# Two 1024 x 1024 projections as streamed seven-product steps, with the weights' sums moved ahead and the residual loaded into the gathering tiles

## The chip, the cores and the metric

The kernel runs on one core of a Trainium2 chip. The metric is the device time of one execution in microseconds; three runs of the kernel before gave 1946.44, 1946.65 and 1947.6 us, a median of 1946.65. Engines: PE is TensorE (PEld its weight loads), DVE is VectorE, ACT is ScalarE, POOL is GpSimd, and SP issues most of the DMAs. All data is float32; the matmuls take operands of the format fp32r.

## The reference

A decoder block: a hybrid mixer (a Mamba-2 branch and a gated linear attention branch, merged by gates), cross-attention to 256 memory tokens, a SwiGLU FFN, with a residual add after each and norms ahead. 1024 tokens, 1024 channels, D_FF 2816. What matters here is the end of the mixer and the beginning of the cross-attention:

```python
merged = sigmoid(g_ssd) * (y_ssd @ w_up_ssd) + sigmoid(g_gla) * (y_gla @ w_up_gla)
h = h + merged @ w_o                               # output projection
n = rmsnorm(h, norm_xattn)
q = (n @ w_xq).reshape(B, S, 4, 256)               # query projection
s = einsum('bshd,bmhd->bhsm', q, k) * 256 ** -0.5  # k, v from the memory, made earlier
o = einsum('bhsm,bmhd->bshd', softmax(s), v).reshape(B, S, 1024) @ w_xo
h = h + o
h = h + (silu(n2 @ w_g) * (n2 @ w_u)) @ w_ffn_out
```

## The kernel before, in words

Activations lie channels x tokens. A float32 product is made from three fp32r matmuls: each operand is split into a high part (`ACT.activation` with Copy) and the rest (a DVE subtraction), and high x high, high x low, low x high are summed in PSUM (`split`).

Large matrix products (input projections, FFN) run in the Strassen-Winograd form: both operands are cut into quarters, seven products B11, B21, T1, B22, T2, T3, T4 of quarters or of sums of quarters give the four quarters of the result. Sums of the down weights `w_ffn_out` are made early by `presum` on POOL: for each of 11 row blocks it loads 1 MB into the one tile `pre`, makes four sums of 128 x 512 and stores each to `down_d`, as steps of a generator that runs beside other stages.

The five projections `w_up_ssd`, `w_up_gla`, `w_o`, `w_xq`, `w_xo` don't use that form. `dense` (called with 0 to 4) walks over 8 blocks of output channels and two halves of the tokens; each of the 16 outputs is one PSUM bank (`acc`) and 8 blocks x 3 matmuls, 384 matmuls of 128x128 by 128x512 in all. Its weights come through `Left`, which loads 1024 x 256 pieces into "aux" slots and splits one block of 128 columns at a time into a ring of two `wd` tiles. Its right operands are eight pairs of high and low tiles (`hl`) that the stage before fills through its `post`:

- `dense(1)` (`w_up_gla`) gates, adds and splits each result into `i_wo` (`post_yg`);
- `dense(2)` (`w_o`) adds the residual, which `quad_of(xT_d)` loads two blocks ahead into tiles `ga`, stores to `h1_d`, scales and splits into `i_xq` (`put_xq`), and squares and adds up for the norm (`s1.take`; POOL or DVE, as `either` chooses by a meter of their queues);
- `dense(3)` (`w_xq`) splits its results into `i_q`. Beside it `s1.close` sums the squares over channels with tiny matmuls, and POOL raises to the power -1/2 (`rstd`), from which the softmax scale `xsc` comes;
- attention goes over 4 heads x 2 token halves (scores, transposes, values) and fills `i_xo`; its keys and values (`kvhl`) are loaded and split by `load_kv`. `dense(4)` (`w_xo`) follows, and then the FFN.

`run(main, (side, rate), ...)` interleaves the program order of a main generator with side generators. The Tile framework then schedules each engine's instructions by priority against its own model of times, with slots allotted as they come free (pools of slots: 14 "op", 4 "aux", 4 "m", each 8 KB a partition); `ahead()` raises the priority. PSUM has four `acc` and four `bank` banks.

## Time and profile before

| | |
|---|---|
| median of three runs | 1946.65 us (1946.44 to 1947.6) |
| profiled execution, first to last instruction | 1949.0 us |
| TensorE busy | 1916.2 us, 98% |
| DVE, ACT, POOL busy | 1298.5, 845.8, 557.8 us |
| granted TensorE clock | 0.998 |
| DMA | 317.98 MB, mean 163 GB/s |
| first matmul of the five projections | 801.9 us |
| attention's first matmul | 1156.5 us |

Durations of matmuls in the profile overlap (they are pipelined, and their ends modelled), so that the time of many matmuls is read from the start of the first to the start of the one after the last. A line of the profile can be a helper's, L73 above all: there the names of the tiles tell operations apart. In an answer by tile, "x40: 1211/1225/2319" are the count and the least, median and greatest duration in ns; in a group, "| 11.9, 1493 |" are busy us and mean ns; in a timeline, the two first numbers are start and duration in us.

### The profile page before, as it was taken

The page shows a single profiled execution, that of the slowest core. Times are in us where ns is not written, and L with a number is a line of the kernel's source. Part 1 is how long each engine was busy: PE and PEld are TensorE (multiplying, and loading weights), DVE is VectorE, ACT ScalarE, POOL GpSimd, SP SyncE. Part 2 cuts the span into 40 slices and gives each one's busy share as a digit, 9 for nine tenths or more (in the row PEclk, how much of TensorE's full clock was granted, in tenths as well). Part 3 has the DMA queues.
Part 4 walks back from the last instruction along what each step waited for, and adds up shares of the span by engine and source line. Part 5 has one row for each costly group of instructions (what it writes and reads, how often), then busy time and mean ns, then how long its engine had stood idle before and what let it go on. Part 6 is the DMA issues. An engine that isn't in the chain of part 4 may idle for free.

```text
span 1949.0 us, 26264 instructions
## 1 busy us (share of the span) xinstructions
PE 1916.2 (98%) x9776; PEld 1615.6 (83%) x9776; DVE 1298.5 (67%) x1873; ACT 845.8 (43%) x1485; POOL 557.8 (29%) x428
## 2 busy tenths in 40 slices
PE   7999999999999999999999999999999999999998
PEld 7998787888878888788887888888888888888888
DVE  7766879877776764655534237677777777766566
ACT  7534564655553444643223235444333333345243
POOL 0012334345543231022433000006445544320002
PEclk9999999999999999999999999999999999999999
DMA  9423383446553653997675201442233224177463
GB/s 341 144 93 101 130 307 107 152 161 186 174 173 123 198 167 124 348 346 270 226 269 164 82 22 44 140 141 82 90 126 110 82 100 144 42 271 239 157 224 126
DMA packets 237875, 317.98 MB, mean 163 GB/s; under 512 B 16538, under 2 KB 156036, under 8 KB 237748
## 3 DMA queue, kind: packets, MB, share of 16 engines
q1 hardware_dynamic: 236020, 310.01, 47.4%
q10 hardware_dynamic: 1728, 6.29, 0.8%
q8 instruction: 77, 1.26, 0.3%
q14 instruction: 50, 0.41, 0.1%
HBM read 215.27 MB, written 100.99 MB: 162 GB/s over the span
## 4 chain that ended last, share of the span: by engine, by line
PE 43%; DMA 3%; POOL 2%; DVE 1%; issue 1%; ACT 1%; POOLq 0%; SPq 0%; DVEq 0%; ACTq 0%
PE acc L51 38%; PE bank L51 4%; DMA pre<-in_w_ffn_out_dram 1%; POOL pre L73 1%; DMA down_d<-pre 1%; PE bank L55 1%; POOL ssum L73 0%; DVE hl L73 0%; POOL sa L73 0%; DMA h_d<-ga 0%; DMA ga<-vm_d 0%; DVE wd L73 0%; ACT wd L227 0%; ACT sq L493 0%; DVE phl L73 0%
## 5 line engine op out<-in xcount | busy, mean ns | idle before, releaser
L51 PE MATMUL acc<-hl,wd 128*128 128x512 f32 x1920 | 440.4, 390 | 3.6 <-DVE wd L73 2.0
L51 PEld LDWEIGHTS acc<-hl,wd 128*128 128x128 f32 x1920 | 359.6, 188 | 80.7 <-DVE wd L73 3.3
L73 DVE TENSOR_TENSOR wlo<-raw,whi 128x512 fp32r<-128x512 f32 x272 | 236.4, 875 | 103.6 <-ACT whi L227 103.5
L227 ACT ACTIVATE whi<-raw 128x512 fp32r<-128x512 f32 x272 | 169.5, 629 | 247.6 <-PE acc L51 201.0
L73 DVE TENSOR_TENSOR o<-acc,o 128x512 f32<-128x512 f32 (+1 forms) x256 | 172.6, 676 | 108.8 <-PE acc L51 95.4
L51 PE MATMUL acc<-fs 128*128 128x512 f32 (+1 forms) x792 | 155.7, 356 | 0.1
L51 PEld LDWEIGHTS acc<-fs 128*128 128x128 f32 x792 | 130.7, 189 | 20.8 <-issue 0.5
L73 DVE TENSOR_TENSOR fs<-fr,fs 128x1024 fp32r<-128x1024 f32 (+1 forms) x84 | 98.9, 1217 | 36.5 <-ACT fs L227 36.4
L227 ACT ACTIVATE fs<-fr 128x1024 fp32r<-128x1024 f32 (+1 forms) x84 | 79.2, 982 | 95.9 <-PE acc L51 31.2
L73 POOL TENSOR_TENSOR raw<-raw,sa 128x512 f32<-128x512 f32 x44 | 57.1, 1297 | 207.8 <-DVE wlo L73 207.8
L73 POOL TENSOR_TENSOR sa<-raw 128x512 f32<-128x512 f32 x43 | 69.6, 1619 | 107.0 <-DMA raw<-in_w_in_dram 78.9
L227 ACT ACTIVATE whi<-sa 128x512 fp32r<-128x512 f32 x96 | 59.6, 626 | 93.7 <-PE acc L51 92.3
L73 DVE TENSOR_TENSOR wlo<-sa,whi 128x512 fp32r<-128x512 f32 x96 | 80.9, 843 | 13.7 <-ACT whi L227 12.7
L73 DVE TENSOR_TENSOR wd<-raw,wd 128x1024 fp32r<-128x1024 f32 x40 | 52.8, 1323 | 47.6 <-ACT wd L227 47.2
L73 POOL TENSOR_TENSOR rstd<-rstd,mhalf 128x4 f32<-128x4 f32 (+1 forms) x7 | 8.7, 1246 | 257.0 <-DVE rstd L73 257.0
L227 ACT ACTIVATE wd<-raw 128x1024 fp32r<-128x1024 f32 x40 | 42.2, 1057 | 90.4 <-PE acc L51 89.8
L51 PE MATMUL acc<-T4h,whi 128*128 128x512 f32 x192 | 76.3, 397 | 2.4 <-DVE o L73 2.4
L51 PE MATMUL acc<-B22h,wlo 128*128 128x512 f32 x192 | 75.7, 394 | 1.5 <-DVE wlo L73 1.5
L51 PE MATMUL acc<-T1h,whi 128*128 128x512 f32 x192 | 76.3, 397 | 0.0
L51 PE MATMUL acc<-T2h,whi 128*128 128x512 f32 x192 | 75.9, 395 | 0.0
L51 PE MATMUL acc<-T3h,whi 128*128 128x512 f32 x192 | 75.9, 395 | 0.0
L51 PE MATMUL acc<-B22h,whi 128*128 128x512 f32 x192 | 75.7, 394 | 0.0
(399 smaller groups left out, 4698.6 us busy)
## 6 DMA issues: line engine op xcount, KB each, us to landing
raw<-in_w_in_dram SPq DMA_DIRECT2D x26, 1024.0 KB, 5.9
raw<-in_w_ffn_in_dram SPq DMA_DIRECT2D x22, 1024.0 KB, 6.5
act_d<-o SPq DMA_DIRECT2D x77, 256.0 KB, 2.1
fr<-act_d SPq DMA_DIRECT2D x35, 512.0 KB, 7.9
pre<-in_w_ffn_out_dram SPq DMA_DIRECT2D x11, 1024.0 KB, 10.0
fr<-down_d SPq DMA_DIRECT2D x20, 512.0 KB, 3.9
down_d<-pre SPq DMA_DIRECT2D x33, 256.0 KB, 3.1
h_d<-ga SPq DMA_DIRECT2D x32, 256.0 KB, 3.1
```

What stands on the lines that cost most here:

```text
L51: return s.e.matmul(o, x, y, **kw)
L55: return s.e.transpose(o, x, i)
L73: return f(*a, **kw)
L227: ACT.activation(hi, src, AF.Copy)
```

## The change

`w_o` and `w_xq` become instances of a new class `Wide`: seven products in the order B11, T1, B22, T2, B21, T3, T4, each of 512 x 512 x 512 quarters over all channels. A product has two steps of 24 matmuls (4 blocks of output rows x 2 blocks of the sum x 3 terms), four PSUM banks at a time. Four `acc` banks keep a running sum from B11 through T2 and T3 to T4; four `bank` banks hold T1 + B22, and then B21. The quarters of the right operand stay in float32 in four `rq` tiles, are combined in place on DVE (`COMB`) and split step by step together with the streamed weights (`ws`). Weights come as 1 MB quarters, either from the matrix or from sums that `presum` now makes for `w_o` and `w_xq` ahead of the down weights (8 steps more; in program order the last 30 of all its sub-steps now stand beside attention). With `base`, the tile that gathers a quarter (`wk`) is first loaded with the residual, and each evacuation adds to it (`scalar_tensor_tensor` with 0.5). `post_yg` and `put_xq` write float32 quarters and no longer split. `kv_side` loads and splits the first head's keys and values beside the query projection; those of the other heads move from "m" to "op" slots. `w_xo` gets a `Left` of its own, started beside the query projection.

```diff
     down_d = dram("down_d", 4 * D_FF // 2, HALF)
+    wos_d = dram("wos_d", 2 * D, HALF)
+    xqs_d = dram("xqs_d", 2 * D, HALF)
     kT_d = dram("kT_d", D, MEM)
...
     JS = (0, 1)
+    class Wide:
+        SEQ = ("B11", "T1", "B22", "T2", "B21", "T3", "T4")
+        LEFT = {"B11": (0, 0), "B21": (0, 1), "T1": 0, "B22": 3, "T2": 1, "T3": 2, "T4": (1, 1)}
+        COMB = {"T1": ((0, 0), (0, 1), (0, 0)), "T2": ((0, 0), (1, 1), (0, 0)), "T3": ((0, 1), (1, 1), (0, 1)),
+                "T4": ((1, 0), (1, 0), (0, 0))}
+        RIGHT = {"B11": (0, 0), "B22": (1, 1), "B21": (1, 0), "T1": (0, 0), "T2": (0, 0), "T3": (0, 1), "T4": (1, 0)}
+        OUT = {"B11": (0, 0), "T1": (1, 1), "B22": (0, 1), "T2": (0, 1), "B21": (0, 0), "T3": (1, 1), "T4": (1, 0)}
+        def __init__(s, W, sums_d, post, keys, side, base=None, scale=1.0, two=None):
+            s.W, s.sums_d, s.post, s.keys, s.side, s.base, s.scale = W, sums_d, post, keys, side, base, scale
+            s.two = two or (lambda ap: DVE)
+            s.q, s.raw, s.ops, s.keep, s.chain = {}, [], [], {}, None
+        def quad(s, i, j):
+            if (i, j) not in s.q:
+                s.q[i, j] = slot("op", (P, 4, HALF), name="rq")
+            return s.q[i, j]
+        def load(s, n):
+            while len(s.raw) < min(n, 7):
+                src = s.LEFT[s.SEQ[len(s.raw)]]
+                if isinstance(src, tuple):
+                    i, j = src
+                    w = s.W[half(j), half(i)]
+                else:
+                    w = s.sums_d[half(src), :]
+                r = slot(s.keys[len(s.raw)], (P, 4, HALF), name="wr")
+                SP.dma_start(r, w.rearrange("(k p) c -> p k c", p=P))
+                s.raw.append(r)
+        def home(s, i, j):
+            if (i, j) not in s.keep:
+                k = s.keep[i, j] = slot(s.side[len(s.keep)], (P, 4, HALF), name="wk")
+                if s.base is not None:
+                    SP.dma_start(k, s.base[half(i), half(j)].rearrange("(u p) c -> p u c", p=P))
+            return s.keep[i, j]
+        def prep(s, n):
+            while len(s.ops) < min(n, 14):
+                m, kp = divmod(len(s.ops), 2)
+                s.load(m + 1)
+                name, c = s.SEQ[m], slice(2 * kp, 2 * kp + 2)
+                x = [slot("op", (P, 2, 2, HALF), F32R, name="ws") for _ in range(2)]
+                with ahead():
+                    if name in s.COMB:
+                        o, a, b = (s.quad(*ij)[:, c] for ij in s.COMB[name])
+                        sub(s.two(o), o, a, b)
+                    split(s.raw[m][:, c], x[0][:, 0], x[0][:, 1])
+                    split(s.quad(*s.RIGHT[name])[:, c], x[1][:, 0], x[1][:, 1])
+                s.ops.append(x)
+        def evac(s, name, u, p):
+            i, j = s.OUT[name]
+            o = p if name == "T4" and s.base is None else s.home(i, j)[:, u]
+            first = name in ("B11", "T1", "B22")
+            with ahead():
+                if s.base is not None:
+                    DVE.scalar_tensor_tensor(o, p, s.scale, o, ALU.mult, ALU.add)
+                elif first:
+                    ACT.activation(o, p, AF.Copy)
+                elif name != "T4":
+                    add(DVE, o, p, o)
+                if not first:
+                    s.post(i, j, u, o)
+        def steps(s):
+            x = 0
+            for m, name in enumerate(s.SEQ):
+                if name in ("B11", "T1", "B21"):
+                    banks = [(acc if name == "B11" else bank)() for _ in range(4)]
+                    if name == "B11":
+                        s.chain = banks
+                elif name in ("T2", "T3", "T4"):
+                    banks = s.chain
+                fresh = name in ("B11", "T1", "B21")
+                if s.base is not None:
+                    for z in s.SEQ[m:m + 2]:
+                        s.home(*s.OUT[z])
+                for kp in range(2):
+                    s.load(m + 3)
+                    s.prep(x + 3)
+                    w, b = s.ops[x]
+                    for u in range(4):
+                        for k in range(2):
+                            for n, (a, c) in enumerate(((0, 0), (0, 1), (1, 0))):
+                                PE.matmul(banks[u], w[:, a, k, u * P:(u + 1) * P], b[:, c, k],
+                                          start=fresh and kp + k + n == 0, stop=kp + k == 2 and n == 2,
+                                          skip_group_check=True)
+                    x += 1
+                    if kp:
+                        for u in range(4):
+                            s.evac(name, u, banks[u])
+                    yield
     class Left:
...
             return s.w[n]
-    left = Left((t["w_up_ssd"], t["w_up_gla"], t["w_o"], t["w_xq"], t["w_xo"]))
+    left = Left((t["w_up_ssd"], t["w_up_gla"]))
     def paired(keys):
...
         split(src, x[:, 0, half(j)], x[:, 1, half(j)], e)
-    def dense(no, ins, post, pre=lambda o, j: None, js=JS):
+    def dense(no, ins, post, pre=lambda o, j: None, js=JS, left=left):
         todo = [(o, j) for o in range(NB) for j in (js if o + 1 < NB else js[::-1])]
...
     EVEN, ODD = ("op",) * 8, ("op",) * 6 + ("aux",) * 2
-    i_ys, i_yg, i_wo, i_xq, i_q, i_xo = (paired(x) for x in (EVEN, ODD, EVEN, ODD, EVEN, EVEN))
+    i_ys, i_yg, i_q, i_xo = (paired(x) for x in (EVEN, ODD, EVEN, EVEN))
     def fetch(src, dst, gain=None):
...
     s1 = Stats(rp)
+    wides = (("w_o", wos_d), ("w_xq", xqs_d), )
     def presum():
         r = slot("m", (P, 2, D), name="pre")
-        for k in range(KP):
-            SP.dma_start(r, t["w_ffn_out"][256 * k:256 * k + 256, :].rearrange("(j p) c -> p j c", p=P))
+        todo = [(t[w].rearrange("(j k p) c -> k p j c", j=2, p=P)[k], d, 4, k) for w, d in wides for k in range(4)]
+        todo += [(t["w_ffn_out"][256 * k:256 * k + 256, :].rearrange("(j p) c -> p j c", p=P), down_d, KP, k)
+                 for k in range(KP)]
+        for src, dst, kn, k in todo:
+            SP.dma_start(r, src)
             yield
...
             s1_ = sums["m"].tile([P, HALF], F32, name="sa", tag="sa", bufs=2)
-            put = lambda n, ap: SP.dma_start(down_d[(n * KP + k) * P:(n * KP + k + 1) * P, :], ap)
+            put = lambda n, ap: SP.dma_start(dst[(n * kn + k) * P:(n * kn + k + 1) * P, :], ap)
             add(POOL, s1_, a(1, 0), a(1, 1))
...
         gated(g, p)
-        add(either(g), g, g, y)
-        into(i_wo, o, j, g)
+        q = wo.quad(o // 4, j)[:, o % 4]
+        add(either(g), q, g, y)
+    def post_wo(i, j, u, q):
+        o = 4 * i + u
+        SP.dma_start(h1_d[o * P:(o + 1) * P, half(j)], q)
+        put_xq(o, j, q, col("norm_xattn", o))
+        s1.take(j, q)
+    wo = Wide(t["w_o"], wos_d, post_wo, ("aux",) * 7, ("m", "m", "m", "aux"), xT_d, 0.5)
+    def wide_side(x, n):
+        for _ in range(n):
+            yield
+        x.load(2)
+        yield
+        x.prep(1)
+        yield
+        x.prep(2)
+        yield
     def residual(store, stats, gain, put, scale=1.0):
...
         return post
+    xq = Wide(t["w_xq"], xqs_d, lambda i, j, u, p: into(i_q, 4 * i + u, j, p), ("aux", "m", "aux") * 3, ("m", "aux", "aux"))
     def put_xq(o, j, q, g):
-        x = hl(i_xq, o)
-        h, l = x[:, 0, half(j)], x[:, 1, half(j)]
-        ACT.activation(h, q, AF.Copy, scale=g)
-        DVE.scalar_tensor_tensor(l, q, g, h, ALU.mult, ALU.subtract)
+        ACT.activation(xq.quad(o // 4, j)[:, o % 4], q, AF.Copy, scale=g)
     def waiting(g, n):
...
     early = presum()
-    run(dense(0, i_ys, post_ys, lambda o, j: gate(gs_d, o, j)), (fetch_gated(yg_d, sr_d, i_yg), 1.0), (waiting(early, 12), 1.0))
-    run(dense(1, i_yg, post_yg, lambda o, j: (gate(gg_d, o, j), quad(ysg_d, o * P, 0, j))), (early, 1.1))
-    run(dense(2, i_wo, residual(h1_d, s1, "norm_xattn", put_xq, 0.5), quad_of(xT_d)), (early, 1.1))
+    run(dense(0, i_ys, post_ys, lambda o, j: gate(gs_d, o, j)), (fetch_gated(yg_d, sr_d, i_yg), 1.0), (waiting(early, 8), 1.0))
+    run(dense(1, i_yg, post_yg, lambda o, j: (gate(gg_d, o, j), quad(ysg_d, o * P, 0, j))), (early, 1.5),
+        (wide_side(wo, 11), 1.0))
+    run(wo.steps(), (early, 1.3))
     kv = []
-    def load_kv(h):
+    def fetch_kv(h):
         es = [rp.tile([P, 2, 256], F32, name="ga", tag="ga") for _ in range(2)]
-        h_ = slot("m" if h < 3 else "op", (P, 2, 4, 256), F32R, name="kvhl")
         SP.dma_start(es[0], kT_d[h * 256:(h + 1) * 256, :].rearrange("(i p) m -> p i m", p=P))
         SP.dma_start(es[1], vm_d[:, h * 256:(h + 1) * 256].rearrange("(i p) c -> p i c", p=P))
+        return es
+    def split_kv(es, pin=lambda x: x):
+        h_ = slot("op" if kv else "m", (P, 2, 4, 256), F32R, name="kvhl")
         for i in range(2):
-            split(es[i], h_[:, 0, 2 * i:2 * i + 2], h_[:, 1, 2 * i:2 * i + 2])
+            pin(ACT.activation(h_[:, 0, 2 * i:2 * i + 2], es[i], AF.Copy))
+            pin(sub(DVE, h_[:, 1, 2 * i:2 * i + 2], es[i], h_[:, 0, 2 * i:2 * i + 2]))
         kv.append(h_)
+    def load_kv(h):
+        split_kv(fetch_kv(h))
     xsc = cp.tile([P, NCH], F32, name="xsc")
...
         yield
-    run(dense(3, i_xq, lambda o, j, p, g: into(i_q, o, j, p)), (xq_side(), 1.0), (early, 1.0))
-    drain(early)
-    load_kv(0)
+    def kv_side():
+        for _ in range(2):
+            yield
+        es = fetch_kv(0)
+        for _ in range(9):
+            yield
+        split_kv(es, pinned)
+        yield
+    left_xo = Left((t["w_xo"],))
+    def next_left():
+        left_xo.upto(2)
+        yield
+    run(xq.steps(), (xq_side(), 1.0), (early, 1.0), (kv_side(), 1.0), (waiting(next_left(), 12), 1.0))
     u_xo_stats = Stats(rp)
...
             a.score(1)
+        for _ in range(3):
+            next(early, None)
+    drain(early)
     rbc2 = u_xo_stats.sum
...
     B = Operands(b_xo, 4, order=("B11", "T1", "B21", "B22", "T2", "T3", "T4"))
-    for n, _ in enumerate(dense(4, i_xo, residual(h2_d, u_xo_stats, "norm_ffn", put_xo), quad_of(h1_d), js=(1, 0))):
+    for n, _ in enumerate(dense(0, i_xo, residual(h2_d, u_xo_stats, "norm_ffn", put_xo), quad_of(h1_d), js=(1, 0), left=left_xo)):
         if n >= 8:
...
         if n == 12:
```

## The prediction

> **What bounds the kernel now.** I read the page's busy shares first, then the 40 slices, then the chain, then the stages by windows.
>
> ```profile
> span 1949.0 us, 26264 instructions
> PE 1916.2 (98%) x9776; PEld 1615.6 (83%) x9776; DVE 1298.5 (67%) x1873; ACT 845.8 (43%) x1485; POOL 557.8 (29%) x428
> PE   7999999999999999999999999999999999999998
> ...
> 1320.48 459.26 PE acc L51 x2026
> ```
>
> TensorE is full in all but the first and last slice, and the chain that ended last runs on it: 2026 matmuls of 512 columns in 459.26 us, 226.7 ns each. That, and not the 390 ns that the groups print (pipelined, ends modelled), is the price of one matmul. The profiled execution (1949.0 us) stands 2.35 us above the median of 1946.65.
>
> The two stages that change are the third and fourth of the five dense projections. Their place on TensorE, by the timeline and the windows (busy us of PE, PEld, DVE, ACT, POOL; then clock, DMA share, GB/s):
>
> ```profile
> 869.68 161.78 PE L51 MATMUL acc<-hl,wd 128*128 128x512 f32 x713
> 1031.84 0.73 PE L51 MATMUL acc<-hl,wd 128*128 128x512 f32 x2 [0.38 <-ACT wd L227]
> 1033.34 21.60 PE L51 MATMUL acc<-hl,wd 128*128 128x512 f32 x94 [0.76 <-DVE wd L73]
> 1055.09 0.73 PE L51 MATMUL acc<-hl,wd 128*128 128x512 f32 x2
> 1056.60 17.97 PE L51 MATMUL acc<-hl,wd 128*128 128x512 f32 x78 [0.78 <-DVE wd L73]
> 1074.73 9.36 PE L51 MATMUL acc<-hl,wd 128*128 128x512 f32 x40 [0.15 <-DVE hl L73]
> ...
> 1087.23 69.42 PE L51 MATMUL acc<-hl,wd 128*128 128x512 f32 x305
> 1156.50 7.96 PE L51 MATMUL acc<-kvhl,hl 128*128 128x256 f32 x65
> L51 PE MATMUL bank<-ones,ssum x16: 164/208/251, 1083.9 to 1087.1; 128*128 128x1 f32 x16
> ```
> ```profile
> 200.00:450.00 250.00, 246.08 (x1206) 201.17 (x1206) 207.06 (x244) 136.91 (x221) 103.78 (x78) 1.00 0.52 176
> 889.00:976.00 87.00, 87.00 (x386) 72.04 (x385) 48.51 (x54) 23.31 (x33) 34.81 (x24) 1.00 0.73 252
> 976.00:1063.00 87.00, 84.93 (x371) 69.09 (x370) 34.67 (x38) 24.58 (x36) 31.27 (x23) 1.00 0.66 220
> 1087.00:1156.00 69.00, 69.00 (x306) 57.14 (x306) 15.43 (x20) 13.05 (x19) 1.01 (x1) 1.00 0.14 46
> 1156.00:1221.00 65.00, 64.61 (x404) 57.16 (x404) 46.03 (x117) 38.81 (x102) 0.00 (x0) 1.00 0.10 33
> 1700.00:1880.00 180.00, 180.00 (x804) 149.01 (x803) 117.13 (x126) 78.85 (x91) 18.56 (x10) 1.00 0.64 221
> ```
>
> Counting back from 1156.5 us, where attention begins, 768 matmuls (two projections of 384) reach to about 977.1 us. The two stages take 179.3 us; 768 x 0.2267 = 174.1 us of it is matmul. Of the other 5.2 us, 1.5 us go to the sixteen tiny matmuls of the statistics (1083.9 to 1087.2 us), and 3.7 us are waits, mostly for a split weight (wd). The granted clock is 1.00. DVE and ACT have much room here before the change: 34.67 and 24.58 us of 87, then 15.43 and 13.05 of 69.
>
> **The change, part by part.**
>
> *Matmuls.* A projection was 8 x 2 outputs x 8 blocks x 3 terms = 384 matmuls. It becomes 7 products x 4 rows x 4 blocks x 3 = 336 of the same form (128x128 stationary, 128x512 moving). Two projections lose 96: 96 x 0.2267 = 21.8 us, all on the path. The old 3.7 us of waits go with the old streaming. Ceiling of the gain: 25.5 us (179.3 - 672 x 0.2267 - 1.5). What takes their place is the question.
>
> [...]
>
> *Operands of the steps.* Each projection has 14 half-products, and each splits 1024 elements a partition of weights and as many of activations: 28 splits. Each T product also combines two quarters first, 2 x 4 = 8 subtractions of the same width, all on DVE.
>
> ```profile
> L227 ACT ACTIVATE wd<-raw x40: 1039/1061/1065, 800.8 to 1275.2; 128x1024 fp32r<-128x1024 f32 x40
> L73 DVE TENSOR_TENSOR wd<-raw,wd x40: 1211/1225/2319, 803.2 to 1276.3; 128x1024 fp32r<-128x1024 f32 x40
> L73 DVE SCALAR_TENSOR_TENSOR ga<-acc,ga 128x512 f32<-128x512 f32 x13 | 8.9, 683 | 12.2 <-PE acc L51 12.2
> L493 ACT ACTIVATE sq<-ga 128x512 f32<-128x512 f32 x10 | 6.2, 622 | 25.2 <-POOL ssum L73 25.2
> L227 ACT ACTIVATE hl<-acc x16: 576/590/602, 1075.5 to 1157.4; 128x512 fp32r<-128x512 f32 x16
> L73 DVE TENSOR_TENSOR hl<-acc,hl x16: 679/686/692, 1076.1 to 1159.3; 128x512 fp32r<-128x512 f32 x16
> L1368 ACT ACTIVATE hl<-ga,cols x16: 707/723/727, 986.0 to 1071.4; 128x512 fp32r<-128x512 f32 x16
> L73 POOL TENSOR_TENSOR ssum<-ssum,sq x14: 1282/1344/1590, 1010.9 to 1072.7; 128x512 f32<-128x512 f32 x14
> ```
>
> Output projection, 76.2 us of matmul (336 x 0.2267). DVE: 28 splits + 8 combinations at 1.225 = 44.1, 28 evacuations at 0.683 = 19.1, together 63.2 us undisturbed. ACT: 28 x 1.06 = 29.7, plus 16 scalings at 0.723 and 16 squares at 0.62, 51 us: no bound. Query projection: DVE 44.1 + 12 additions from PSUM (8.2) + 16 splits of the result at 0.686 (11.0) + the first keys' two (1.4) = 64.7 us; ACT 28 x 1.06 + 12 copies and 16 splits at about 0.59 = 46 us. So DVE rises from about 40% to about 84% of these stages before any disturbance. The gated projection before them loses its 16 splits of i_wo (11 us of DVE) and gets the first two half-products' operands (5 us).
>
> *The sums' POOL work.* Sums of w_o and w_xq add 8 steps of four POOL additions to the 11 of the down weights; every step also issues 1 load and 4 stores on SP, 40 issues more in all at 0.32 to 0.43 us spread over 300 us, and 16 MB of traffic.
>
> ```profile
> 833.98 1.28 POOL L73 TENSOR_TENSOR sa<-pre 128x512 f32<-128x512 f32 x1 [47.69 <-DMA pre<-in_w_ffn_out_dram]
> L73 POOL TENSOR_TENSOR pre<-pre x22: 1272/1733/2359, 836.6 to 1025.6; 128x512 f32<-128x512 f32 x22
> 956.87 2.16 POOL L73 TENSOR_TENSOR sa<-pre 128x512 f32<-128x512 f32 x1 [8.56 <-issue]
> ...
> 1005.81 1.28 POOL L73 TENSOR_TENSOR sa<-pre 128x512 f32<-128x512 f32 x1 [14.29 <-DMA h_d<-ga]
> ```
>
> The first step's sums start at 834 us. Four steps start from 956.87 to 1005.81, three periods of 16 us; a single buffer makes load, sums and stores take turns. The first steps are slower (834, 865, 893 us), and 16 more periods from 893 reach about 1155: beside attention, where POOL is idle (0.00 of 65 us). The sums of w_o are done by about 915 us, 60 us before use; those of w_xq by about 980, 80 us before use. Cost on the path: 0, with that cover. Takes and the small power on POOL queue behind a step's 5.2 us; the softmax scale waits for them and has some 40 us to spare (under PSUM below).
>
> What POOL does to DVE is not free:
>
> ```profile
> 944.85 3.46 POOL L73 TENSOR_TENSOR pre<-pre 128x512 f32<-128x512 f32 x2
> 947.07 2.32 DVE L73 TENSOR_TENSOR wd<-raw,wd 128x1024 fp32r<-128x1024 f32 x1
> L73 DVE TENSOR_TENSOR wd<-raw,wd 128x1024 fp32r<-128x1024 f32 x8 | 11.9, 1493 | 0.2 <-ACT wd L227 0.2
> ```
>
> A split of 1.225 us took 2.32 beside POOL, and the mean in the gated stage (889 to 976, POOL busy 40%) was 1.493. The new stages put 36 such subtractions in 76 us beside about 30 us of sums and, in the first, 14 takes (19 us). At +0.27 us each DVE would need 73 us in the first and 74 in the second, at 1.5 times that disturbance 78 and 77. Against 76.2 that is just full; two half-products are prepared before the first stage starts.
>
> Stall from this, bounded: below 0 us (1700:1880, streamed operands of the same build, no loss at 65% DVE); above 12 us (rival 1). Between: 200:450, where DVE is 83% busy, lost 3.9 of 250 us, 1.6%, or 2.4 us on 152. I take twice that, 5 us, since DVE comes out fuller here than there.
>
> *PSUM.* Four banks hold the running sum from B11 to T4, four serve T1/B22 and B21. B22 writes T1's banks and T4 writes T3's, so each waits for an evacuation; between a bank's last matmul and its next lie 18 matmuls, 4.1 us, against 0.68 us of evacuation and at most one or two operations ahead of it. Taken as 0; it costs if DVE runs late, which the 5 us hold. The statistics' matmuls now find no free bank until B22 ends, 33 us into the query stage: what waits for them is the scale, needed 43 us on.
>
> *Residual in the gathering tiles.* 16 quarter-block loads become 4 loads of 1 MB, at least 7 us ahead of need; a buffer for the first comes free 11 us before the gated stage ends. 0.
>
> *Traffic.* Output stage: weights and sums 7, residual 4, h1 4, sums' steps about 9 MB, 24 MB in 76 us, 315 GB/s, against 220 now.
>
> ```profile
> GB/s 396 402 405 380 397 385 396 404 407 310 218 242 186 332 290 253 246 238 367 119 236 223 314 218 158 231 319 210 188 323 377 215 229 344 309 115 142 159 54 187
> pre<-in_w_ffn_out_dram SPq DMA_DIRECT2D x11, 1024.0 KB, 10.0
> ```
>
> This row (800 to 1063) shows about 400 GB/s sustained at its start, so 315 fits, and a 1 MB operand that lands in 10 us is asked for three products (33 us) ahead. Bounds 0 and 2 us (the first stage starts its sums earlier in the full part); I take 0.
>
> *Boundaries.* B11 and T1 need only the upper channels, finished half a stage earlier; each later quarter is ready two products before use. Attention's first head needs the quarters of T2 and B21. Gain or loss 0, to 5 us of loss (rival 2). Beside attention POOL now runs: DVE's 46 us of 65 mostly read PSUM; 0 to 2 us, taken 0.
>
> Sum: -21.8 - 3.7 + 5 = -20.5 us: 1949.0 becomes 1928.5, and the median 1926.2.
>
> **The rivals.**
>
> 1. *DVE and POOL take turns and DVE becomes the bound.* If every two-input subtraction and every POOL addition exclude one another, the first stage needs 44.1 + 18 (14 takes at 1.285) + 25.7 (five steps of four) = 87.8 us of turns, 11.6 over; the second 45.5 + 25.7 = 71.2, none over. With the 2.4 us as above the gain is 11.5: 1935.1. For it: the 2.32 us row. Against it: in the gated stage the measured delay was 0.27 us, not a whole POOL operation, and sums can slip, as nobody waits for them. [...]
>
> 2. *Handover to attention.* The scores need acc banks, all held to T4's end, and T4 is evacuated through 4 splits behind T3's 8 DVE operations (8 x 0.686 = 5.5 us). If TensorE waits this out, 1931. Against: those have 10.9 us of T4 itself to drain.
>
> 3. *Slower: SP's queue.* SP issues in order, and a store of a sum waits for POOL; the 14.29 us row shows POOL itself held 14 us by a store. If a product's operand can be issued only once a step (16 us) and a product lasts 10.9, 14 products lose 14 x 5.1 = 71 us: 1926 + 71 - 5 = 1992. It decides from 1.8 us a product (25.5 / 14). Against: the same queue with the same steps cost 3.7 us in the window before, and operands are asked for three products ahead.
>
> 4. *No gain:* the freed TensorE time returns as waits of 20 us or more, 1946.
>
> **How the numbers follow.** Forecast 0.60, rival 1 0.20, rival 2 0.09, rival 3 0.07, rival 4 0.04 (mostly within 0.2%, about what a measurement of this kernel can tell from no change). The likeliest case's own range is 1921 (no stall) to 1931; the range of 8 in 10 reaches from 1920.5 to 1937 to take in rivals 1 and 2. Faster 0.90, same 0.03, slower 0.07.
>
> **What would show it.** 672 matmuls of the new form, 226 to 228 ns apart, in 154 to 162 us between the gated projection and the scores; DVE near 90% there with split means of 1.4 to 1.6 us; TensorE waits on splits or evacuations of 3 to 8 us in total; the sums' last POOL operation between 1120 and 1190 us. It is wrong if TensorE's waits in these stages pass 12 us, if one product waits for its operand's DMA, or if attention takes over 68 us.

## The result, and the profile after

The changed kernel is slower: 1965.59 us (median of four, 1955.8 to 1969.61) against 1947.12 us of the kernel before beside it; ratio 1.0082, 95% interval 1.0055 to 1.0109. The forecast was 1926.2 us. The profiled execution is the fastest of the four, 1955.8 us with a span of 1954.1, so its rows show less than the usual loss; e0 below shows a usual one.

The profile after: totals, and the slices of TensorE, the granted clock and POOL.

```profile
span 1954.1 us, 26262 instructions
PE 1902.8 (97%) x9680; PEld 1599.1 (82%) x9680; DVE 1382.9 (71%) x1927; ACT 881.4 (45%) x1521; POOL 609.0 (31%) x454
PE   7999999999999999999997999999999999999998
POOL 0012333345443221023235540006444444320002
PEclk9999999999999999999999998999999999999999
```

The 96 matmuls are gone (9776 to 9680), and TensorE is no longer full in slice 22 (1026 to 1075 us). By stage, from first matmuls (profiled executions): up to the streamed stages 974.8 us against 977.1 (-2.3); the two streamed stages 184.3 against 179.4 (+4.9); attention and `w_xo` 143.2 against 140.5 (+2.7); the rest 651.8 against 652.0. The matmuls alone would fill 153.8 us of the 184.3 (672 at 0.2267 us, and 1.5 us of statistics). TensorE's timeline there (start, duration, in brackets the idle time ahead and what ended it):

```profile
974.82 8.32 PE L51 MATMUL acc<-ws 128*128 128x512 f32 x36
...
998.23 0.49 PE L51 MATMUL acc<-ws 128*128 128x512 f32 x1 [1.49 <-ACT ws L229]
1000.91 3.03 PE L51 MATMUL acc<-ws 128*128 128x512 f32 x8 [2.19 <-DVE ws L73]
...
1055.57 14.03 PE L51 MATMUL acc<-ws 128*128 128x512 f32 x51 [8.55 <-ACT sq L495]
1071.07 0.50 PE L51 MATMUL acc<-ws 128*128 128x512 f32 x1 [1.47 <-DVE wk L73]
...
1145.32 12.70 PE L51 MATMUL acc<-ws 128*128 128x512 f32 x48 [3.54 <-DVE wk L73]
1159.12 6.12 PE L51 MATMUL acc<-kvhl,hl 128*128 128x256 f32 x49 [1.10 <-DVE hl L73]
```

The largest stop, 8.55 us ahead of the output projection's T4, is put down to ACT's squares. The four engines just before it:

```profile
1047.60 2.28 DVE L73 TENSOR_TENSOR ws<-rq,ws 128x1024 fp32r<-128x1024 f32 x1
1048.76 3.46 POOL L73 TENSOR_TENSOR pre<-pre 128x512 f32<-128x512 f32 x2
...
1052.18 1.26 POOL L73 TENSOR_TENSOR ssum<-ssum,sq 128x512 f32<-128x512 f32 x1
1053.47 0.63 ACT L495 ACTIVATE sq<-wk 128x512 f32<-128x512 f32 x1 [5.89 <-POOL ssum L73]
1054.13 0.69 DVE L73 TENSOR_TENSOR ssum<-ssum,sq 128x512 f32<-128x512 f32 x1 [4.25 <-ACT sq L495]
1054.74 1.28 DVE L73 SCALAR_TENSOR_TENSOR wk<-acc,wk 128x512 f32<-128x512 f32 x2
```

A take is the addition of a square to the norm's sum. Read upward: the evacuation of T3 at 1054.74 stands on DVE behind a take; that take waits for ACT's square, and the square for the only `sq` tile, which a take on POOL still reads; the take on POOL stands behind a step of the sums. TensorE waits for POOL through two engines.

Windows of the same trace (length; busy us of PE, PEld, DVE, ACT, POOL; clock, DMA share, GB/s):

```profile
974.80:1159.10 184.30, 164.05 (x689) 131.74 (x687) 144.06 (x135) 88.64 (x118) 91.77 (x54) 0.94 0.74 265
1159.10:1302.30 143.20, 141.14 (x737) 119.46 (x738) 93.70 (x186) 71.01 (x154) 5.10 (x4) 1.00 0.29 96
1047.00:1056.00 9.00, 0.45 (x2) 0.46 (x2) 4.75 (x5) 2.35 (x4) 6.88 (x5) 0.65 1.02 364
1056.00:1062.00 6.00, 6.00 (x19) 4.71 (x19) 1.92 (x4) 4.00 (x7) 3.13 (x3) 0.68 1.01 352
1062.00:1068.00 6.00, 6.00 (x28) 4.96 (x27) 3.31 (x4) 3.19 (x5) 3.28 (x4) 1.00 0.50 191
```

The fourth row is the tail of the stop: 19 matmuls in 6 us where 26 fit, at a granted clock of 0.68. This stop of 8.6 us costs 1.7 us more by its tail, and in the fifth row the clock is back at 1.00. All waits of TensorE in the two stages add up to 20.3 us. The first row gives the rest of the loss: its matmuls keep TensorE busy for 164.05 us at a clock of 0.94, where 153.8 would do, and these 10.2 us are in the main the tails of all the stops together. Behind the smaller stops the same trace has a clock of 0.95 from 1004 to 1016 us, 0.85 from 1074 to 1084 and 0.78 from 1146 to 1152.

### The profile page after: what moved, and what is told of

Its sections match the earlier page's. It is cut to its first block, busy times and chain, and to the rows that moved or that the text cites. A ratio compares the mean times of both kernels' runs of the same rounds, so it can differ in the third digit from the quotient of the medians.

```text
span 1954.1 us, 26262 instructions
## 1 busy us (share of the span) xinstructions
PE 1902.8 (97%) x9680; PEld 1599.1 (82%) x9680; DVE 1382.9 (71%) x1927; ACT 881.4 (45%) x1521; POOL 609.0 (31%) x454
## 4 chain that ended last, share of the span: by engine, by line
PE 42%; DMA 2%; DVE 2%; POOL 2%; issue 2%; ACT 0%; POOLq 0%; DVEq 0%; SPq 0%; ACTq 0%
PE acc L51 36%; PE bank L51 6%; DMA pre<-in_w_ffn_out_dram 1%; POOL pre L73 1%; DMA down_d<-pre 1%; DVE ws L73 1%; PE bank L55 1%; DVE hl L73 0%; POOL ssum L73 0%; POOL sa L73 0%; DVE wk L73 0%; DVE kvhl L73 0%; DVE wd L73 0%; DVE yt L73 0%; DMA xqs_d<-pre 0%
## 5 line engine op out<-in xcount | busy, mean ns | idle before, releaser
L229 ACT ACTIVATE whi<-raw 128x512 fp32r<-128x512 f32 x272 | 169.5, 629 | 251.0 <-PE acc L51 207.2
L51 PE MATMUL acc<-hl,wd 128*128 128x512 f32 x1152 | 263.8, 390 | 1.9 <-ACT wd L229 1.4
L51 PEld LDWEIGHTS acc<-hl,wd 128*128 128x128 f32 x1152 | 215.5, 188 | 48.4 <-ACT wd L229 2.6
L51 PE MATMUL acc<-ws 128*128 128x512 f32 x384 | 96.4, 410 | 18.4 <-ACT sq L495 8.6
L51 PEld LDWEIGHTS acc<-ws 128*128 128x128 f32 x384 | 75.8, 199 | 37.1 <-ACT sq L495 8.9
L73 POOL TENSOR_TENSOR sa<-pre 128x512 f32<-128x512 f32 x19 | 28.0, 1472 | 231.2 <-DMA pre<-in_w_o_dram 94.3
```

The source lines that it names most:

```text
L51: return s.e.matmul(o, x, y, **kw)
L73: return f(*a, **kw)
L229: ACT.activation(hi, src, AF.Copy)
```

## The experiments

Theories: *coupling* (POOL's sums hold products up, by way of SP's queue and of the square tile), *DVE* (it is simply full), *traffic* (DMA is full). In the expectations, A is the coupling by the square tile and D the one by SP's queue, B is DVE, and C is a late operand at the first stage's start. "Stages" are the two streamed stages, "attention" is attention and `w_xo`; both are us of the one profiled execution, which can stand apart from the median: by 9.8 us below it in after, and by 9.4, 4.8 and 3.8 us above it in e7, e8 and e10.

| kernel | median | ratio to before, 95% | stages | attention |
|---|---|---|---|---|
| before | 1947.12 to 1949.48 beside the others | | 179.4 | 140.5 |
| after | 1965.59 | 1.0055 to 1.0109 | 184.3 | 143.2 |
| after again (e0) | 1966.1, one | | 192.3 | 143.2 |
| e1 takes on DVE | 1965.6 | 1.0072 to 1.0107 | 191.7 | 143.2 |
| e2 no sums | 1939.74 | 0.9938 to 0.9968 | 167.3 | 143.3 |
| e3 sums later | 1948.97 | 0.9990 to 1.0009 | 168.3 | 151.7 |
| e4 = e3 + e1 | 1941.57 | 0.9946 to 0.9976 | 161.1 | 150.5 |
| e5 only `w_o` | 1955.47 | 1.0023 to 1.0050 | 185.6 | 140.0 |
| e6 only `w_xq` | 1954.47 | 1.0012 to 1.0041 | 94.7, query alone | 143.1 |
| e7 = e1 + own queue | 1950.23 | 0.9991 to 1.0024 | 167.7 | 154.3 |
| e8 = after + own queue | 1957.42 | 1.0033 to 1.0067 | 169.5 | 155.8 |
| e9 = e4 + own queue | 1949.16 | 0.9991 to 1.0011 | 154.2 | 159.1 |
| e10 = e4 + stores on own queue | 1948.35 | 0.9986 to 1.0006 | 162.6 | 158.3 |
| e11, few beside attention | 1941.06 | 0.9945 to 0.9969 | 160.4 | 150.9 |
| e12 = e11 + own queue | 1957.28 | 1.0023 to 1.0052 | 154.2 | 160.6 |
| e13 = e4 + softmax scale on ACT | 1937.48 | 0.9918 to 0.9945 | 161.2 | 141.9 |
| e14 = e4, no sums | 1936.52 | 0.9915 to 0.9940 | 164.7 | 143.1 |

**e2, the sums' POOL work taken away.** The kernel leaves out the 44 additions of the down weights: their steps store what they loaded, with the same bytes on the same queue.

```diff
+            if dst is down_d:
+                for n in range(4):
+                    SP.dma_start(dst[...], a(n // 2, n % 2))
+                    yield
+                continue
```

> Leaves out POOL's four sums in each of the 11 steps of the down weights (the pieces are stored as loaded, same bytes, so the FFN's last product is not the reference's); the sums of w_o and w_xq stay. Theory A: POOL's takes no longer stand behind sums, gain 10 to 13 us, about 1953. Theory B: DVE's subtractions fall from up to 2.3 us to 1.22 us, and the query stage's stops (about 6 us) go as well: A and B together about 1945 to 1948. Theory C: 6 us at the start of the first stage stay, since the traffic is the same; without C about 1940.

e2 is 26 us faster than after and 5 us below what A and B together were expected to bring, though DMA moves more per second in the stages (304 GB/s against 265). POOL's 44 additions, which nobody reads for 500 us, decide the sign. One stop of 6.95 us stays, at 1004, for the first stage's third operand.

**e1, the takes on DVE.**

```diff
-                    add(either(q), dst, dst, q)
+                    add(DVE if s.on_dve else either(q), dst, dst, q)
```

> The adds of the squares for the norm in these two stages go to DVE alone (14 adds), POOL keeps only the sums of weights. Theory A (one square tile shared by takes on POOL and on DVE: an evacuation on DVE stands behind an add that waits for ScalarE's square, which waits for POOL's take, which stands behind the sums): the 8.6 us stop ahead of T4 and the slow clock after it go, 10 to 13 us, so about 1953 against the changed kernel's 1965.6. Theory B (DVE is over-full because POOL's sums block its two-input subtractions): DVE gets 5 us more to do, no gain, 1965 or more. Theory C (operands of the first stage land late): the 6 us at the stage's start stay in any case.

The stop ahead of T4 goes, and a longer one appears in the query stage, so that the time stays at 1965.6 us. POOL, DVE, SP, ACT and TensorE in e1's timeline:

```profile
1067.57 17.10 POOL L73 TENSOR_TENSOR sa<-pre 128x512 f32<-128x512 f32 x1 [13.35 <-DMA h_d<-wk]
1084.74 1.30 POOL L73 TENSOR_TENSOR pre<-sa,pre 128x512 f32<-128x512 f32 x1
```
```profile
1082.30 1.22 DVE L73 TENSOR_TENSOR ws<-rq,ws 128x1024 fp32r<-128x1024 f32 x1
```
```profile
1059.86 2.18 SPq L1465 DMA_DIRECT2D h_d<-wk  x4
1084.69 0.32 SPq L1412 DMA_DIRECT2D down_d<-sa  x1
...
1091.88 0.38 SPq L1223 DMA_DIRECT2D wr<-in_w_xq_dram  x1
```
```profile
1099.60 1.06 ACT L229 ACTIVATE ws<-wr 128x1024 fp32r<-128x1024 f32 x1 [18.73 <-DMA wr<-in_w_xq_dram]
```
```profile
1101.19 4.11 PE L51 MATMUL bank<-ws 128*128 128x512 f32 x11 [14.42 <-ACT wk L1255]
```

A POOL addition of 1.3 us lasted 17.10. DVE ran two-SBUF-input operations without a break from 1066 on; the last began at 1082.30 and took 1.22, and POOL ended 1.15 us behind it: one addition. Meanwhile the sum's store stood at the head of SP's queue, SP issued nothing for 22 us, and a product's weights, queued behind that store, were asked for at 1091.88. ACT waited for them until 1099.60; the evacuation `wk` that the last row names stands behind that split on ACT, and TensorE stood still for 14.42 us.

**e0, the changed kernel again**, unedited.

> The changed kernel once more, for a second trace: its profiled execution (1955.8 us) was the fastest of its four times, the others 1964 to 1968. Theory 'queue': the missing 10 us are a stop of 10 to 15 us in the query stage, with a single POOL addition of 10 us or more and a weight operand issued only behind its store, as with the takes on DVE; then this execution, if it is slow, shows such a stop. Theory 'spread': no new stop, but all of the present ones (8.6, 3.5, 2.2 us) a few us longer and a lower clock. A time near 1955 with the known stops tells nothing.

At 1966.1 us it stands with the slower three of the first four, and it shows the long addition without any edit:

```profile
L73 POOL TENSOR_TENSOR sa<-pre x19: 1278/1291/13874, 830.6 to 1169.6; 128x512 f32<-128x512 f32 x19
```

(the first trace's greatest is 2354). SP issued nothing from 1092.8 to 1111.3. The stop itself was shorter than expected, 5.38 and 1.73 us, with a clock of 0.53 from 1138 to 1146 us. The stop ahead of T4 is there too, 7.91 us.

**e5 and e6, one projection alone.** The other one stays in the old form.

```diff
-wides = (("w_o", wos_d), ("w_xq", xqs_d), )
+wides = (("w_o", wos_d), )      # e5;  e6: (("w_xq", xqs_d), )
```

> Only the output projection is streamed; the query projection is as before the change. 48 matmuls fewer (10.9 us) than the kernel before. Theory B (DVE over-full beside POOL's sums) and theory C: the output stage loses what it lost in the changed kernel (about 5 us at its start, 10 us ahead of T4), so 1948 to 1954, no gain over the kernel before. If the two stages only fail together (DVE never gets even), about 1940.

> Only the query projection is streamed; the output projection is as before, where DVE is 40% busy. 48 matmuls fewer, 10.9 us. Theory B: the query stage alone has DVE at about 85% undisturbed beside one sums' step in 15 us, it loses 2 to 6 us: 1941 to 1945. Theory D (a sum's store on SP's queue waits for POOL, POOL is shut out by DVE's row of two-input subtractions, and operands wait behind that store: the 14.4 us stop of the run with the takes on DVE): a stop of this kind can come here too, then 1950 or more.

Each alone is slower than before. e5 has the first mechanism (6.04 us ahead of T4, by way of POOL's take), e6 the second: a POOL addition of 10.10 us in a row of DVE subtractions, the store behind it, and a stop of 15.04 us. Attention stays at 140.0 us in e5 and is 143.1 in e6, as in the changed kernel (143.2), so these 2.7 us come with the streamed query projection.

```profile
1077.39 10.10 POOL L73 TENSOR_TENSOR sa<-pre 128x512 f32<-128x512 f32 x1 [7.49 <-DMA pre<-in_w_ffn_out_dram]
```
```profile
1102.11 4.17 PE L51 MATMUL bank<-ws 128*128 128x512 f32 x11 [15.04 <-ACT wk L1255]
```

**e3 and e4, the same work at another time.** In program order the sums of `w_o` and `w_xq` stand sooner (rate 2.0), no step of the down weights stands beside the streamed stages, and their 55 sub-steps were meant for attention and `w_xo`, with a second load tile. e4 adds e1's edit.

```diff
-    run(wo.steps(), (early, 1.3))
+    run(wo.steps())
-    run(xq.steps(), (xq_side(), 1.0), (early, 1.0), ...
+    run(xq.steps(), (xq_side(), 1.0), ...
```

> No step of the down weights beside the two stages: w_o and w_xq are summed beside the gated projections, the down weights from attention to the next projection, with two load tiles from the third round on. Takes stay where they were. Theories A and B: both causes are gone, about 1945 as for the run without POOL's sums. Theory C: the first stage has 9 MB less traffic and no store ahead of its operands in the queue, so 6 us more, about 1935 to 1940. If attention suffers from POOL, its stretch (143 us from the first score to the FFN in the changed kernel) grows by what is missing.

> The two edits together: sums of the down weights later, and the takes on DVE alone. Theory A: with no sums on POOL the chain through POOL costs at most a take (1.3 us), so within 3 us of the run with the sums later. [...] If it is over 4 us faster, ScalarE's and DVE's waiting for POOL's takes is a cost of its own.

The traces differ from the program order: in both, three steps of the down weights still run in the output projection, where their loads were free to go (POOL is busy for 26.46 us from 976.2 to 1060 us in e4), and none runs beside the query projection. In e4 the stages have only two stops, 1.91 and 2.03 us near their start, and e4 beats both kernels. e3 against e4 isolates the takes (7.2 us of stage time). But attention pays: 150.5 us against 143.

**e7 to e10, the sums' DMAs on POOL's own queue** (e10 the stores alone).

```diff
-            SP.dma_start(r, src)
+            nc.gpsimd.dma_start(r, src)
-            put = lambda n, ap: SP.dma_start(...)
+            put = lambda n, ap: nc.gpsimd.dma_start(...)
```

> Takes on DVE as in the first run, and the loads and stores of the sums are issued from POOL's own queue in place of SP's. Theory D: no operand waits behind a sum's store, so the 14.4 us stop and its slow clock go, and the 4 us at the first stage's start with them: 1965.6 - 20 = about 1943 to 1947. Theory B alone: DVE is as full as before, POOL has more to do, 1965 or more.

> The changed kernel with the sums' DMAs on POOL's own queue, the takes as they were (either engine). Theory D alone: about 1950, since the stop ahead of T4 through the takes (8.6 us) stays and the queue's stops go. Theory A and D both at work: 5 to 12 us slower than the run with both edits. Theory B alone: 1965 or more.

> e4 (sums later, takes on DVE), and the sums' loads and stores issued from POOL's queue, not SP's. Theory 'queue': the two stops that e4 keeps at the start of the output projection (1.9 and 2.0 us, with a slow clock behind them, 5 to 6 us together) come from the third operand that stands behind sums' stores on SP; they go, and the time falls by 4 to 6 us to 1936 to 1938. Theory 'traffic': they come from DMA engines that are full there (the early sums beside the gated projection); the time stays at 1940 to 1943, or the gated projection gets longer.

> e4, and the sums' stores alone issued from POOL's queue, the loads still from SP. Theory 'queue': the loads into the single tile wait for the stores to land, so SP is still held, but only till POOL is through, not behind it: half of the gain of e9, 1937 to 1941. Theory 'traffic': no difference from e4, 1940 to 1943.

The start of the first stage is clean in e7 to e10. Its third operand is asked for at 981 to 983 us there, against 986.69 in after and 995.42 in e2, with the DMA engines as full (share 1.04 in e10 from 986 to 1000 us, 1.02 in after), so SP's queue made it late. e8 is 7.2 us slower than e7, as A and D together would have it; yet e8's own trace has no stop ahead of the output projection's T4, so there the takes are not seen at work.

The own queue has a price that no theory had. In the runs where SP issues the sums' DMAs, no DVE operation on the tiles `ws`, `rq`, `ssum`, `hl`, `kvhl`, `phl`, `wd`, `wk`, `pe` or `mx` lasts over 2.35 us between 970 and 1310 us. In the five runs where POOL issues them, or the stores alone (e7 to e10, e12), the longest lasts 5.4 to 6.6 us. In e10:

```profile
1051.50 5.15 DVE L73 TENSOR_TENSOR ssum<-ssum,sq 128x512 f32<-128x512 f32 x1 [1.31 <-ACT sq L495]
1054.82 1.28 POOL L73 TENSOR_TENSOR pre<-pre 128x512 f32<-128x512 f32 x1
...
1058.44 0.79 PE L51 MATMUL acc<-ws 128*128 128x512 f32 x1 [3.67 <-DVE wk L73]
```

A take of 0.69 us on DVE lasts 5.15: it ends 0.55 us behind the last of the step's four POOL additions, and an evacuation and TensorE wait behind it. e7 and e8 keep 14 and 16 us over the floor; their longest stops, 4.00 and 5.15 us, are put down to DVE and stand behind such holds. e10, at 1948.35 us, is outside what either of its theories allowed. Why DVE waits for a whole step when POOL issues DMAs between its additions was not tested.

In e9, with two steps of the down weights still beside the output projection, nothing at all is left to wait for in the stages:

```profile
981.70:1135.90 154.20, 154.20 (x689) 127.91 (x688) 128.42 (x144) 87.99 (x117) 21.41 (x20) 1.00 0.53 181
1135.90:1200.70 64.80, 53.99 (x337) 47.58 (x335) 52.92 (x105) 31.20 (x89) 27.32 (x30) 0.95 0.30 110
```

154.2 us against a floor of 153.8, clock 1.00. Yet e9 is no faster than before, where 'queue' expected 1936 to 1938: the stages begin 5.5 us later than e4's, and attention takes 159.1 us. For the first, TensorE waits 4.21 us for the first weight of the gated projections, which SP asks for at 800.58 us against 796.30 in e4; the sums' first load left POOL's queue ahead of it, at 786.53 us (819.48 from SP in e4), but that this load is the reason was not tested. The second row shows the other: TensorE is busy for 53.99 of 64.8 us, and POOL, which was idle there before the change, for 27.32.

**e11 and e12, fewer sums beside attention** (10 sub-steps in place of 40 in program order, the rest beside `w_xo`; e12 with the own queue).

```diff
-        for _ in range(4):      # an iteration of attention
+        for _ in range(1):
-        for _ in range(2):      # a step of w_xo
+        for _ in range(3):
```

> e4 (sums later, takes on DVE) with the 55 sub-steps of the down weights' sums shared out otherwise: 10 beside attention (one an iteration instead of four) and 45 beside the w_xo projection (three a step instead of 15 in all). Theory 'attention pays': the 10 us that attention and w_xo take more than before (150.5 against 140.5) are POOL beside the softmax's short DVE chain; with a quarter of it there, 6 to 8 us come back and the time is 1934 to 1936. Theory 'they cost wherever they stand': the w_xo projection, whose splits are two-input subtractions too, takes as much as attention gives, 1940 to 1944.

> The same division with the sums' loads and stores on POOL's queue (e9 with 10 and 45 sub-steps). In e9 the two streamed projections took 154.2 us, their floor, yet attention and w_xo 159.1 and the gated projections 5 us more. Theory 'attention pays': attention and w_xo fall from 159.1 to about 145, the time to 1934 to 1937. Theory 'they cost wherever they stand': 1946 to 1950 as in e9.

Neither decides anything: the scheduler let POOL run as many additions beside attention as before (e11 24.89 us of POOL in the first 64.8, e4 24.70), since their loads were free to go. e12 also pushed sums into the FFN, which took 660.7 us in place of 652.

**e13 and e14, who pays in attention.** e14 leaves the 44 down additions out of e4, as e2 does. e13 computes everything, and moves one softmax operation from DVE to ACT:

```diff
-                DVE.tensor_scalar(s.e[...], s.e[...], sm[:, a:a + 1], None, ALU.mult)
+                ACT.activation(s.e[...], s.e[...], AF.Copy, scale=sm[:, a:a + 1])
```

> e4 (sums later, takes on DVE) with the softmax's 32 scalings of 128x256 done by ACT in place of DVE. Theory 'attention pays': e4's attention and w_xo take 150.5 us against 143.3 where POOL sums nothing, because a DVE scaling that reads only SBUF waits for POOL's additions (up to 1.45 us in e4, 6.1 in e9); ACT was not seen slowed by them, so some 4 to 7 us come back: 1935 to 1938. Theory 'other': the loss is the traffic or the order of attention's work, or the tiny one-column operations of DVE are held as long, and 32 scalings more on ACT bring nothing: 1940 to 1944.

> e4 with the down weights' pieces stored unsummed (their 44 POOL additions are left out, so the FFN's last product is not the reference's; loads, stores and their places stay). Theory 'attention pays': attention and w_xo fall from 150.5 to about 143, the time to 1933 to 1936. Theory 'traffic': loads and stores cost it, 1940 to 1943.

Both bring attention back, to 143.1 (e14) and 141.9 us (e13). The operation concerned, by tile, in the kernel before, in e4, in e9 and in e14 (least, median, greatest ns):

```profile
L73 DVE TENSOR_SCALAR pe<-pe,sm x32: 341/348/355, 1163.1 to 1201.3; 128x256 f32<-128x256 f32 x32
```
```profile
L73 DVE TENSOR_SCALAR pe<-pe,sm x32: 344/353/1450, 1141.3 to 1195.7; 128x256 f32<-128x256 f32 x32
```
```profile
L73 DVE TENSOR_SCALAR pe<-pe,sm x32: 342/350/6110, 1140.0 to 1198.1; 128x256 f32<-128x256 f32 x32
```
```profile
L73 DVE TENSOR_SCALAR pe<-pe,sm x32: 343/349/355, 1144.1 to 1187.5; 128x256 f32<-128x256 f32 x32
```

The scaling has one SBUF tile as input. Beside POOL's additions it took up to 1.45 us in e4, and up to 6.11 in e9, where POOL issues the DMAs as well and TensorE waited 5.86 us for what stands behind it on DVE. e14 shows that the additions cost attention its 7 us. e13 shows less: moving the scalings also takes some 11 us of work off DVE (32 x 0.348, an estimate), its attention is 1.2 us shorter than that of e14, which has no such additions, and the move was not tried in a kernel without them. At 1937.48 us, 0.7% below before, e13 is the fastest version that computes everything. It gives 5.7 us back in the FFN (1279.1 to the end at 1936.8, 657.7 against 652), where DVE is busy for all of the first 20.9 us; that was not followed up.

**m1 and m2, POOL beside a row of DVE subtractions by itself.** No layer; rows of 14 and 18 subtractions of 128x1024 without a break, four POOL additions released within the row, by DVE (m1) or by a load (m2).

> No layer at all (the output is a copy of inputs): seven sections, each a row of 14 DVE operations of 128x1024 and four POOL additions of 128x512 from SBUF that the row's third operation releases (in section 4 POOL's first runs ahead of the row). 1: two-SBUF-input subtractions without a break. 2: a PSUM-reading addition after every fourth. 3: a one-input operation of 512 after every fourth. 4: POOL first. 5: each subtraction waits for ACT. 6: one-input operations. 7: additions that read PSUM. Theory 'shut out': a row that never waits keeps POOL out until it ends or reads PSUM: POOL's first addition lasts 11 to 14 us in section 1, 2 to 6 in 2, about 2.4 at most in 5 and 7, and in section 4, where POOL has the first turn, they alternate (DVE 2.3 us, POOL 2.2 us each). Theory 'turns': they alternate in every section, no POOL addition over 2.5 us; then the 17.1 and 10.1 us additions of e1 and e6 have another cause, such as DMA.

> No layer again (the output is a copy): nine rows of 18 two-SBUF-input DVE subtractions of 128x1024 without a break; POOL's four additions wait for a load that is issued after the row's second operation and lands within it, as the sums' additions did. In rows 2 to 5 and 8 to 9 a POOL copy of 32 to 256 elements stands ahead of them, to shift their start against the row's beat; in rows 7 to 9 the subtractions are splits with ACT's high parts. Theory 'release by a load' (or theory 'beat'): POOL's first addition lasts to the row's end, 8 us or more, in all rows (in some of them). Theory 'turns': no addition over 2.5 us in any, and what shuts POOL out in the kernel is not in these rows; then it stays open.

In every row of two-SBUF-input subtractions they take turns. POOL's additions (m1, then m2, by tile), and m1's operations on DVE, the last two of them a row with one SBUF input and a row that reads PSUM:

```profile
L75 POOL TENSOR_TENSOR pp<-f,b x24: 1255/2176/2250, 10.5 to 147.2; 128x512 f32<-128x512 f32 x24
```
```profile
L96 POOL TENSOR_TENSOR pp<-r x36: 1294/2239/2255, 12.3 to 239.3; 128x512 f32<-128x512 f32 x36
```
```profile
L53 DVE TENSOR_TENSOR w<-a,b x58: 1209/1219/2285, 6.9 to 142.5; 128x1024 fp32r<-128x1024 f32 x58
L123 DVE TENSOR_SCALAR w<-a x9: 680/682/1755, 126.0 to 135.1; 128x1024 fp32r<-128x1024 f32 x9
L126 DVE TENSOR_TENSOR w<-bank,a x9: 685/687/689, 143.6 to 148.4; 128x512 fp32r<-128x512 f32 x9
```

No addition passes 2.255 us, and a subtraction that meets one takes up to 2.285 in place of 1.219: each waits for about one whole operation of the other. A scaling with one SBUF input is held too (1.755 us in place of 0.682), and one input from PSUM is not (0.685 to 0.689). 'Shut out' fell here: the 9 to 17 us additions of e0, e1, e6 and e8 were not reproduced, neither by what releases POOL nor by its moment. What makes a row hold POOL off for six to fourteen operations stays open; that these additions ended about 1.15 us, one addition, behind the row's last two-SBUF-input operation is seen in the four traces, not tested apart. No row had POOL issue DMAs, so the opposite hold of e7 to e10 was not tried either.

## Why the prediction was wrong

*Matmuls: right.* 96 went, and e9 runs the 672 with their statistics in 154.2 us; 154.2 less 1.5, over 672, is 227 ns.

*The old 3.7 us of waits go: right*, as e9 shows. The ceiling of 25.5 us is there: 179.4 less 154.2 is 25.2.

*DVE: right in size.* It is busy for 144.06 us in both stages; the prediction had 147 to 155 with the disturbance (157 by its own terms, as 64.7 + 36 x 0.405 is 79 and not 77), and 127.9 without, where e9 measures 128.42 with some 10 us of takes on DVE among them. The work alone is not the bound: e9 has no stop with it.

*"Takes ... on POOL queue behind a step's 5.2 us", "Cost on the path: 0, with that cover": the step that failed.* The prediction asked who reads the sums, and nobody does in these stages; it did not ask what stands behind a waiting store on SP, nor which tile a waiting take holds. The weights of products stood behind the store (14.42 us in e1, 15.04 in e6), and evacuations behind the take (8.55 us in after). Without POOL's sums the same kernel gains 26 us (e2).

*PSUM 0, "at most one or two operations ahead of it": failed.* One operation was enough, since it waited for ACT, and ACT for POOL: the 8.55 us ahead of T4.

*Traffic 0: failed by some 5 us.* "Asked for three products ahead" did not hold for the first stage's third operand, which was issued at 986.69 us behind stores of sums, and split at 996. Bandwidth by itself was not it: e10 has no stop there with the DMA engines as full (share 1.04, against 1.02 in after).

*Stall 5 us: mis-sized.* 184.3 less 153.8 is 30.5 us in the profiled execution, 38.5 in e0. The stops make 20.3 us of the 30.5, more than the 12 that the prediction named as a sign of being wrong; the other 10.2 are in the main the slow clock behind them, for which its sum has no term.

*Boundaries, 0 to 2 us beside attention: failed by a little*, 2.7; with e2 and e14, which have no sums there, at 143.3 and 143.1, it isn't POOL. It comes with the streamed query projection (e6 has it, e5 does not); its cause stays open. But the sums did cost 7 us and more wherever they were put beside attention (e3, e4, e9): "mostly read PSUM" was true of DVE's time and not of the one operation in the chain.

*The rivals.* Rival 3, SP's queue, had a chance of 0.07 and named one of the two mechanisms; the other, the square tile, was in no rival, and it makes the largest stop of the profiled execution. Rival 3's price, 5.1 us on each of 14 products, did not come: a few single stops did. It decides from 1.8 us a product; the measured loss, with the square tile's part and the slow clock, was 30.5 / 14 = 2.2 in the profiled execution and 2.75 in e0. The evidence against it, "the same queue with the same steps cost 3.7 us in the window before", came from stages whose DVE was busy 34.67 of 87 us, so that POOL was never held long (the longest of these additions before the change took 2.36 us). Rival 1's turns are real, about one whole operation each (in m1 a subtraction of 1.219 us takes up to 2.285); they did not set the time of the changed kernel, but the longest stops left in e7 and e8 stand behind DVE operations held by POOL for more than a turn. Rival 2's handover cost 1.10 us in after.

## What to carry to other kernels

Work that "nobody waits for" still holds its queue and its tiles, and holds up DVE (a split of 1.22 us took up to 2.32 in after): for each wait it makes, ask what is queued behind it on that engine, and behind the DMA that waits for it. Before a stage is made denser on one engine, look for a queue that carries both its operands and a background job's stores, and give the two different times or different queues; look also at what the second queue's engine shares with the stage, as the sums' DMAs on POOL's queue freed SP and held DVE for up to 6.6 us (e7 to e10). Measure the stage's floor and each neighbouring stage separately: e9 reached the floor and gained nothing, as the same background work was paid for next door.

## What the runs showed of the hardware that was not expected

- A POOL addition of 1.3 us beside an unbroken row of two-SBUF-input DVE operations lasted 17.10, 13.87, 10.10 and 8.94 us (e1, e0, e6, e8), while in m1 and m2 the two took turns at 2.2 us.
- The reverse: a DVE scaling with one SBUF input of 128x256 (0.348 us) lasted up to 1.45 us beside POOL's additions (e4), and up to 6.11 and 6.61 us where POOL issued DMAs between them (e9, e10); so did subtractions and additions with two SBUF inputs (5.29 us in e7, 5.84 in e8, 5.15 in e10), against at most 2.35 us wherever SP issued them.
- After a stop of 8.6 us TensorE's granted clock was 0.68 over the next 6 us and 1.00 over the 6 us behind these; behind e0's stop of 5.38 us it was 0.53 over 8 us, a second stop of 1.73 us among them. Over the two stages TensorE lost 10.2 us in this way, in the main, beside 20.3 us of waiting.
